# Where a gate, a residual and the conditioning dot products are computed in a macaron layer

## The chip, the cores and the metric

The kernel runs on one core of a Trainium2 chip. The metric is the time of one execution in microseconds (us). Before the change it is 1509.61 us, the median of three runs (1508.7 to 1509.68). The engines have these names in the profile: PE multiplies matrices (PEld is its weight load), DVE is the vector engine, ACT the scalar engine, POOL the GpSimd engine, and SP issues most of the DMA transfers. Each engine carries out its own list of instructions in order; an instruction that waits holds up what stands behind it in its list.

## The reference

512 latent tokens `x` and 256 context tokens `ctx`, 1024 channels each, go through a half-step SwiGLU network (FFN1), then two mixers (neighbourhood attention and a gated delta network), then a second half-step network. Each step is modulated by a conditioning vector:

```python
mod_x = (jax.nn.silu(c) @ w_ada + b_ada).reshape(bsz, N_MOD, 1, d)       # 9 vectors of 1024
mod_c = (jax.nn.silu(c_ctx) @ w_ada + b_ada).reshape(N_MOD, 1, d)

def ffn_sublayer(h, m, i, w_up, w_down):
    shift, scale, gate = sub_mod(m, i)
    y = swiglu(modulate(h, shift, scale), w_up, w_down)
    return post_ln(DEEPNORM_ALPHA * h + 0.5 * gate * y, ln_g[i], ln_b[i])

x = ffn_sublayer(x, mod_x, 0, ffn1_w_in, ffn1_w_out)
ctx = ffn_sublayer(ctx, mod_c, 0, ffn1_w_in, ffn1_w_out)
```

What the change touches is how the modulation vectors (`silu(c) @ w_ada`) get computed beside other work, and where `ALPHA * h + 0.5 * gate * y` is formed for FFN1.

## The kernel before

All weights are fp32 in memory. A weight tile of 128x1024 (512 KB) is loaded into a raw buffer `wr` (or `ra`, `rb`), rounded by ACT to `wh` (line 137, the cast) and its remainder is taken by DVE as `wl` (line 139, the lo half). A product is then three matmuls: `wh` by the high half of the data, `wh` by its low half, `wl` by the high half (lines 192 to 194 for the up products and the projections, 211 for the down products).

The stages, in the order of the trace:

- **FFN1 x**: the first units of the up product, 512 tokens wide, to about 112 us.
- **FFN1 c**: the same units for the context, 256 tokens wide (loop `for f in range(N1)` with `ffn_unit`), 118 to 169 us.
- **down1 x, down1 c**: the first part of the down product for 4 tiles of latent tokens and 2 of context tokens (`down`), to 234.6 us. Its sums leave PSUM in the loop at lines 574 to 590: for each token tile the tokens are loaded, DVE multiplies the two banks with the gate (line 588) and adds ALPHA times the tokens (line 589), and the result is stored to `accd`.
- **Seven**: the remaining 14 units of the up product, x and c together, as 7 block products each (class `Seven`). `prep_a` splits the block `ra` (for products 1 and 2), `prep_s` forms sums of `ra` and `rb` (for 5 and 6, and 3 after `prep_3`), `prep_b` the difference (for 7 and 4). The halves of `prep_a` live in the pool `wx` with one buffer each: the next unit's can be written only when products 1 and 2 of this unit have read them. To about 440 us.
- **down2 x, down2 c**: the rest of the down product; `evac1` adds the sums to `accd` read back as `accx` and `x1c`. To about 563 us. FFN1's layer norms (`finish1`) lie beside down2 c.
- **projections**: first four units of `z`, 512 wide, to 589 us, then units of the mixers to 740 us; then scans, attention and FFN2.

The conditioning vectors are dot products: `ada_gen` loads a 512 KB row block of `w_ada` transposed and DVE multiplies it by a row of silu(c) and sums it (line 280, `dot_cols`), once for `x` and, for the sections 2 to 4, once more for `c`. One `ada_step` is one such load with its one or two dots. The raw buffers of these loads come from the rings of the stage, `raw1` in FFN1 and down1, `raw2` in Seven, a pool `ada1` of four buffers in down2 x. In all there are 48 steps in sections 2 to 7: 10 lie in FFN1 x, FFN1 c and down1 x, 25 in Seven (`ADA2`), the last 13 in down2 x (`ADA3`). When a section is done `rows_out` transposes gates to rows and stores them; the gate of FFN1 (section 2) must be there before down1's sums leave PSUM.

A scheduler lays the program's statements out into each engine's list, so that the order in the lists differs from that of the code; `issue_after` only keeps an instruction behind a named one. The weight stream `Stream` uses the pool `wp` with two raw buffers `wr`, two `wh` and two `wl`; Seven's `rb` is one of the same two raw buffers.

## Time and profile before

| | us |
|---|---|
| median of three runs | 1509.61 |
| the profiled execution's own time | 1512.61 |
| its span from the first to the last instruction | 1510.8 |
| PE busy | 1441.6 |
| DVE busy | 1149.5 |
| ACT busy | 662.8 |

The profiled execution is 3.0 us longer than the median and 1.8 us longer than its own span. In the views, one row is one instruction or a few equal ones beside each other: start, length, engine, line, operation, what it writes and reads, and in brackets how long the engine was idle just before it and what ended that. A matmul's own length includes the time in which it overlaps the next one, so the cadence is read from starts.

### The profile page before, as it was taken

To read this page: it belongs to the slowest core of one execution; us is meant where nothing else is said; L and a number is where in the kernel's file an instruction comes from. 1 tells how busy PE (TensorE), PEld (TensorE's weight loads), DVE (VectorE), ACT (ScalarE), POOL (GpSimd) and SP (SyncE) were. 2 spreads that over 40 slices of the span, in tenths; PEclk is the share of its full clock that TensorE was granted. 3 is DMA by queue.
4 is the path that set the end of the run, shared out by engine and by line. 5 is a ranking of instruction groups with operands and counts; after the bars stand their busy time and mean duration, and the time that the engine had idled before them with its cause. 6 is when DMAs were issued, how large, how long until landed. Compare 5 with 4: busy or idle time off the path is not lost.

```text
span 1510.8 us, 23895 instructions
## 1 busy us (share of the span) xinstructions
PE 1441.6 (95%) x9117; PEld 1262.9 (84%) x9117; DVE 1149.5 (76%) x1975; ACT 662.8 (44%) x1090; POOL 211.2 (14%) x262
## 2 busy tenths in 40 slices
PE   6998999999999989999996998989999999999997
PEld 4778989999997778889875777867778999998886
DVE  8787869999988665778677795567669699886626
ACT  5433524434333386555534334267526454444310
POOL 1000000000000110313201001333221022220001
PEclk9999999999999999999998999999999999999999
DMA  9677664445469444222576514274344143233732
GB/s 375 207 262 232 209 236 171 156 164 167 165 231 397 157 153 134 92 78 91 175 214 183 168 64 124 72 261 146 100 168 144 60 136 107 98 112 121 269 98 83
DMA packets 114948, 248.56 MB, mean 165 GB/s; under 512 B 35145, under 2 KB 50577, under 8 KB 114833
## 3 DMA queue, kind: packets, MB, share of 16 engines
q1 hardware_dynamic: 110192, 229.40, 45.4%
q0 software_dynamic: 3056, 12.33, 2.2%
q10 hardware_dynamic: 1586, 5.32, 0.9%
q8 instruction: 71, 1.16, 0.3%
q14 instruction: 43, 0.35, 0.1%
HBM read 215.50 MB, written 31.50 MB: 163 GB/s over the span
## 4 chain that ended last, share of the span: by engine, by line
PE 69%; DVE 13%; DMA 10%; issue 4%; ACT 3%; POOL 1%; SPq 1%; DVEq 0%; ACTq 0%; POOLq 0%
PE ps L211 15%; PE ps L533 4%; PE ps L535 4%; PE ps L534 4%; PE pm L192 4%; PE pm L193 4%; PE pm L194 4%; PE ps L193 3%; PE ps L192 3%; PE ps L1679 3%; PE ps L194 3%; PE ps L1680 3%; PE ps L1681 3%; PE pc L1049 2%; DVE wl L139 2%
## 5 line engine op out<-in xcount | busy, mean ns | idle before, releaser
L139 DVE TENSOR_TENSOR wl<-wr,wh 128x1024 fp32r<-128x1024 f32 (+1 forms) x184 | 226.8, 1238 | 119.2 <-ACT wh L137 119.0
L137 ACT CAST wh<-wr 128x1024 fp32r<-128x1024 f32 (+1 forms) x184 | 185.9, 1015 | 265.7 <-PE pm L193 60.1
L192 PE MATMUL pm<-uxh,wh 128*128 128x512 f32 x320 | 132.4, 414 | 1.0 <-ACT spill L798 1.0
L194 PE MATMUL pm<-uxh,wl 128*128 128x512 f32 x320 | 127.2, 397 | 0.3 <-DVE wl L139 0.3
L193 PE MATMUL pm<-uxl,wh 128*128 128x512 f32 x320 | 127.1, 397 | 0.0
L211 PE MATMUL ps<-wh,hx 128*128 128x512 f32 x352 | 96.1, 391 | 0.9 <-ACT wh L137 0.9
L211 PEld LDWEIGHTS ps<-wh,hx 128*128 128x128 f32 x352 | 65.9, 188 | 15.3 <-ACT wh L137 1.3
L280 DVE SCALAR_TENSOR_TENSOR adap<-wr,crow 128x1024 f32<-128x1024 f32 x61 | 74.6, 1223 | 2.3 <-DMA wr<-in_w_adaT_dram 1.7
L192 PE MATMUL ps<-uh,wh 128*128 128x256 f32 (+1 forms) x208 | 68.6, 331 | 5.0 <-ACT wh L137 5.0
L194 PEld LDWEIGHTS pm<-uxh,wl 128*128 128x128 f32 x320 | 61.1, 191 | 14.3 <-DVE wl L139 1.3
L192 PEld LDWEIGHTS pm<-uxh,wh 128*128 128x128 f32 x320 | 61.5, 192 | 12.6 <-ACT spill L798 1.4
L193 PEld LDWEIGHTS pm<-uxl,wh 128*128 128x128 f32 x320 | 61.4, 192 | 10.6
L114 POOL TENSOR_TENSOR rs<-ve,mhalf 128x1 f32<-128x1 f32 (+2 forms) x46 | 48.2, 1050 | 140.7 <-DVE ve L110 138.3
L193 PE MATMUL ps<-ul,wh 128*128 128x256 f32 (+1 forms) x208 | 67.5, 326 | 0.0
L194 PE MATMUL ps<-uh,wl 128*128 128x256 f32 (+1 forms) x208 | 66.6, 325 | 0.0
L193 PE MATMUL ps<-uxl,wh 128*128 128x256 f32 (+1 forms) x192 | 61.6, 324 | 2.1 <-DVE uxl L139 2.1
L192 PE MATMUL ps<-uxh,wh 128*128 128x256 f32 (+1 forms) x192 | 60.7, 323 | 1.6 <-ACT uxh L137 1.4
L194 PE MATMUL ps<-uxh,wl 128*128 128x256 f32 (+1 forms) x192 | 61.1, 321 | 0.0
L137 ACT CAST wh<-ra 128x1024 fp32r<-128x1024 f32 x31 | 32.6, 1053 | 58.1 <-PE ps L534 20.2
L533 PE MATMUL ps<-ur,wh 128*128 128x384 f32 x168 | 56.5, 336 | 0.0
L534 PE MATMUL ps<-ur,wh 128*128 128x384 f32 x168 | 56.4, 336 | 0.0
L533 PE MATMUL ps<-uh,wh 128*128 128x384 f32 x168 | 56.4, 336 | 0.0
(498 smaller groups left out, 4264.4 us busy)
## 6 DMA issues: line engine op xcount, KB each, us to landing
wr<-in_w_adaT_dram SPq DMA_DIRECT2D x64, 512.0 KB, 4.8
wr<-in_up_dram SPq DMA_DIRECT2D x56, 512.0 KB, 3.7
wr<-in_win_dram SPq DMA_DIRECT2D x52, 512.0 KB, 3.4
wr<-in_dn_dram SPq DMA_DIRECT2D x51, 512.0 KB, 4.0
ra<-in_up_dram SPq DMA_DIRECT2D x24, 512.0 KB, 4.2
rb<-in_up_dram SPq DMA_DIRECT2D x18, 512.0 KB, 3.3
ra<-in_w_adaT_dram SPq DMA_DIRECT2D x16, 512.0 KB, 5.0
wr<-in_w_o_dram SPq DMA_DIRECT2D x8, 512.0 KB, 4.5
```

The costliest lines, as they stand in the source:

```text
L114: G.tensor_tensor(rs[:], ve[:], mhalf[:, 0:n], ALU.pow)
L137: S.copy(hi, src)
L139: marks["lo"] = V.tensor_tensor(lo, src, hi.bitcast(F32), ALU.subtract).ins
L192: T.matmul(ps, a, uh[:, k, :], start=(k == 0), stop=False)
L193: T.matmul(ps, a, ul[:, k, :], start=False, stop=False)
L194: marks["mm"] = T.matmul(ps, b, uh[:, k, :], start=False, stop=(k == nk - 1)).ins
L211: T.matmul(banks[t][d][:, c0:c1], a[:, sl], b[:, d * 512 + c0:d * 512 + c1], start=first and j == 0, stop=last and j == 2)
L280: V.scalar_tensor_tensor(pr[:], raw[:], 1.0, crow, op0=ALU.mult, op1=ALU.mult, accum_out=col[:, c:c + 1])
L533: T.matmul(ps[:], a, mh, start=k == 0, stop=False)
L534: T.matmul(ps[:], a, ml, start=False, stop=False)
L535: T.matmul(ps[:], b, mh, start=False, stop=k == 3)
L1679: T.matmul(ps[:], a, uh[:, k], start=k == 0, stop=False)
```

## The change

Three things change together.

1. The sums of down1 leave PSUM by two plain ACT copies for a token tile and go to `accd` without gate and residual. The blend (`acc*gate`, then `ALPHA*tokens + that`, two DVE instructions over 1024 columns) is done where they are read back: four token tiles in down2 x, in `h_next`, and two context tiles in down2 c, in `between`, whose tokens are loaded there.
2. The 48 steps are spread otherwise: none in FFN1 x and FFN1 c, two in down1 x, six in down1 c (`t_dots`), 18 in Seven (`ADA2`), 8 in down2 x (`ADA3`), and the last 14 in the projections: two after each `z` unit, then one after every second unit. There the raw buffers are the weight stream's own two (`wp`, `wr`), and the row is a broadcast copy `arow`.
3. The gate's row is stored in the fifth unit of Seven; `ada1` has two buffers in place of four.

```diff
-    ADA2 = (2, 1, 2, 1, 2, 1, 2, 2, 2, 2, 2, 2, 2, 2)
-    ADA3 = (2, 2, 2, 2, 2, 2, 2, 2)
+    ADA2 = (2, 1, 1, 2, 1, 1, 2, 1, 1, 2, 1, 1, 1, 1)
+    ADA3 = (1,) * 8
...
         for k in range(KC * (f - F0), min(KC * (f - F0 + 1), KT)):
             modulate_k(pp, "c", k)
-        ada_step(1 + (f == N1 - 1))
...
         ffn_unit(tp, pp, ws.get(), ws.get(), uch, ucl, NCT, *hc[-1])
-        ada_step(f in (0, 2))
-    rows_out(tp, "fs", 2)
...
-        if j == 0:
-            load_g(0)
+
+    def t_dots(j):
+        if j > 1:
+            ada_step()
...
     for kind, n, hs in (("x", 4, hx), ("c", 2, hc)):
-        if kind == "c":
-            load_g(1)
-        banks, tail = down(pp, ws, hs, n, 2 if kind == "x" else 0, tail if kind == "c" else (), between=t_sums if kind == "x" else None)
+        banks, tail = down(pp, ws, hs, n, 2 if kind == "x" else 0, tail if kind == "c" else (), between=t_sums if kind == "x" else t_dots)
...
-            nc.sync.dma_start(xr, tok_src(kind, t))
-            tmp = tl(tp, [P, D], "adap")
             for d in range(2):
-                sl = slice(d * 512, (d + 1) * 512)
-                V.tensor_tensor(tmp[:, sl], banks[t][d][:], g[d][:], ALU.mult)
-                V.scalar_tensor_tensor(xr[:, sl], xr[:, sl], ALPHA, tmp[:, sl], op0=ALU.mult, op1=ALU.add)
+                S.copy(xr[:, d * 512:(d + 1) * 512], banks[t][d][:])
             nc.gpsimd.dma_start(accd[t + 4 * (kind == "c")], xr)
...
         ada_step(ADA2[f], "h")
+        if f == 4:
+            with tc.issue_after(marks["mm"]):
+                rows_out(sgp, [8, P], "row")
...
-        if j > 3:
+        if 0 < j < 5:
+            xrs.append(tl(ad, [P, D], "xr", 3))
             with tc.issue_after(marks["raw"]):
-                nc.sync.dma_start(accx[j - 4][:], accd[j - 4])
+                nc.sync.dma_start(accx[j - 1][:], accd[j - 1])
+                nc.sync.dma_start(xrs[j - 1][:], tok_src("x", j - 1))
+        if 2 < j < 7:
+            blend(accx[j - 3], xrs[j - 3], gx)
         ada_step(ADA3[j])
 
+    def blend(acc, tok, g):
+        with tc.issue_after(marks["lo"]):
+            V.tensor_tensor(acc[:], acc[:], g[:], ALU.mult)
+            V.scalar_tensor_tensor(acc[:], tok[:], ALPHA, acc[:], op0=ALU.mult, op1=ALU.add)
...
-    ada_tp[0], ada_raw[0] = ad, lambda: tl(ad, [P, D], "wr", 4)
+    ada_tp[0], ada_raw[0] = ad, lambda: tl(ad, [P, D], "wr", 2)
...
-    for _ in ada:
-        pass
...
     def between(j):
+        if j in (4, 7):
+            t = j // 7
+            raw = tl(wp, [P, D], "wr", WB)
+            nc.sync.dma_start(raw[:], tok_src("c", t))
+            blend(x1c[t], raw, gc)
...
+    arow = tl(ga_, [P, D], "arow")
+    nc.gpsimd.dma_start(arow[:], sild.broadcast_to([P, D]))
+    rows_of[0], ada_raw[0] = lambda w: arow[:], lambda: tl(wp, [P, D], "wr", WB)
...
     for m in range(4):
         for _ in fill_spill(ga_, "z", m, zd):
             pass
+        ada_step(2)
...
             if 0 <= j - lag < len(units):
                 next(units[j - lag], None)
+        if j % 2:
+            ada_step()
```

How the lists of the engines change is shown at three places. A row has its place in the engine's list, the line of the kernel it belongs to (lines of the changed kernel are up to ten further on than those of before), the operation, what it writes and reads, and what it waits for besides its place.

**DVE, from the end of down1 c into the first unit of Seven, before.** `ra_2140`, `wr_2141` are the blocks `ra`, `rb` of the first unit, `ra_2144` is `ra` of the second; `s_1649` are the sums; 514, 515, 520 and 525 form them.

```order
257 L514 TENSOR_TENSOR s_1649<-wr_2141 128x512 [waits DMAHW6_49]
258 L139 TENSOR_TENSOR wl_2095<-ra_2092,wh_2094 128x1024 [waits DMAHW0_49,Activation_49]
259 L139 TENSOR_TENSOR wl_2113<-ra_2110,wh_2112 128x1024 [waits DMAHW2_49,Activation_49]
260 L515 TENSOR_TENSOR s_1649<-s_1649,ra_2140 128x512 [waits DMAHW0_49,DVE_49]
...
263 L139 TENSOR_TENSOR wl_2149<-ra_2140,wh_2148 128x1024 [waits Activation_49]
264 L139 TENSOR_TENSOR wl_2155<-s_1649,wh_2154 128x1024 [waits Activation_49]
...
274 L139 TENSOR_TENSOR wl_2225<-ra_2144,wh_2224 128x1024 [waits PE_49,Activation_49]
```

The same place after: `ra_2094`, `wr_2095` belong to the first unit, `ra_2098` to the second; 280 is a dot.

```order
233 L139 TENSOR_TENSOR wl_2103<-ra_2094,wh_2102 128x1024 [waits DMAHW6_49,Activation_49]
234 L280 SCALAR_TENSOR_TENSOR adap_2070,colx_72<-wr_2068,crow_83 128x1024 [waits DMAHW4_49,DVE_49]
235 L280 SCALAR_TENSOR_TENSOR adap_2072,colc_73<-wr_2068,crow_83 128x1024 [waits DVE_49]
...
240 L139 TENSOR_TENSOR wl_2171<-ra_2098,wh_2170 128x1024 [waits DMAHW1_49,PE_49,Activation_49]
241 L515 TENSOR_TENSOR s_1589<-wr_2095 128x512 [waits DMAHW3_49]
242 L516 TENSOR_TENSOR s_1589<-s_1589,ra_2094 128x512 [waits DVE_49]
243 L526 TENSOR_TENSOR wr_2095<-ra_2094,wr_2095 128x512
244 L521 TENSOR_TENSOR s_1589<-ra_2094,s_1589 128x512 [waits DVE_49]
245 L139 TENSOR_TENSOR wl_2109<-s_1589,wh_2108 128x1024 [waits Activation_49]
```

The second unit's `prep_a` (row 240, before row 274) has come ahead of the first unit's sums and of their lo half; row 240 waits, through its cast on ACT, for PE's products 1 and 2 of the first unit.

**PE at the same place after.** Product 2 (`ps_2157`) reads `wh_2102`; the products 5 and 6 (`ps_2174`, `ps_2188`) are the next in the list.

```order
1130 L534 MATMUL ps_2157<-uh_88,wh_2102 128x384
1131 L535 MATMUL ps_2157<-ul_89,wh_2102 128x384
1132 L536 MATMUL ps_2157<-uh_88,wl_2103 128x384
1133 L534 MATMUL ps_2174<-ur_1634,wh_2108 128x384 [waits Activation_49]
1134 L535 MATMUL ps_2174<-ur_1634,wh_2108 128x384
1135 L534 MATMUL ps_2188<-ur_1637,wh_2108 128x384
```

Nothing stands between the last matmul of product 2 and the first that needs the sums.

**SP and DVE in the `z` units, after.** `wr_5248` is the weight of the last `z` unit, `wr_5289` and `wr_5354` those of the next two units; 298 and `in_w_adaT` are loads for dots. The two buffers alternate, so `wr_5242` and `wr_5248` have the same one. First SP:

```order
216 L298 DMA wr_5242<-in_w_adaT_dram 128x1024 [waits DMAHW5_49,DVE_49]
...
226 L806 DMA zd_5141<-spill_5279 128x512 [waits DMAHW1_49,DVE_49]
227 L174 DMA wr_5248<-in_win_dram 128x1024 [waits DMAHW2_49,DVE_49]
228 L298 DMA wr_5283<-in_w_adaT_dram 128x1024 [waits DMAHW3_49,DVE_49]
...
230 L298 DMA wr_5286<-in_w_adaT_dram 128x1024 [waits DMAHW5_49,DMAHW2_49,DVE_49]
231 L174 DMA wr_5289<-in_win_dram 128x1024 [waits DMAHW6_49,DVE_49]
```

Then DVE, where 805 is the end of a `z` unit's sums, 887 a row of the mixers' constants and 280 the dots:

```order
634 L805 SCALAR_TENSOR_TENSOR spill_5279<-spill_5279,ps_5254 128x512 [waits Activation_49]
635 L887 TENSOR_SCALAR aex_5187<-aex_5187 128x8 [waits Activation_49]
636 L280 SCALAR_TENSOR_TENSOR wr_5242,colx_72<-wr_5242,arow_5205 128x1024 [waits DMAHW7_49,DMASW7_49]
637 L280 SCALAR_TENSOR_TENSOR wr_5245,colx_72<-wr_5245,arow_5205 128x1024 [waits DMAHW2_49]
...
639 L805 SCALAR_TENSOR_TENSOR spill_5320<-spill_5320,ps_5295 128x512 [waits DMAHW0_49,Activation_49]
640 L139 TENSOR_TENSOR wl_5251<-wr_5248,wh_5250 128x1024 [waits DMAHW2_49,PE_49,Activation_49]
641 L280 SCALAR_TENSOR_TENSOR wr_5283,colx_72<-wr_5283,arow_5205 128x1024 [waits DMAHW3_49,DVE_49]
```

The last `z` unit's weight is loaded behind the first of the two dots (row 636) that read its buffer, and that dot stands behind rows 634 and 635. Before, these weights followed one another in SP's list with no load for a dot between them.

More of the change, by code (lines that the diff above doesn't have):

```diff
@@ L288, in spread_crow, with ada_gen @@
             S.activation(r[:, w, d * 512:(d + 1) * 512], ps[d][:], AF.Silu)
-    def ada_gen(tps, raw_of, crow):
+    rows_of = [lambda w: crow[:, w]]
+    def ada_gen(tps, raw_of):
         for sec in range(2, 8):
@@ L298, in ada_gen @@
                     for w, col in which:
-                        dot_cols(tps[0], raw, crow[:, w], col, sec * 8 + k, sec > 4)
+                        dot_cols(tps[0], raw, rows_of[0](w), col, sec * 8 + k, sec > 4)
                 if k < KT - 1:
@@ L444, in body, with rows_out @@
     ada_tp, ada_raw, rows_due = [tp], [raw1], []
-    ada = ada_gen(ada_tp, ada_raw, crow)
-    def rows_out(p, tag, bufs):
+    ada = ada_gen(ada_tp, ada_raw)
+    def rows_out(p, shape, *tag):
         while rows_due:
-            to_row(tl(p, [P, 512], tag, bufs)[0:8, 0:P], pp, *rows_due.pop(0))
+            to_row(tl(p, shape, *tag)[0:8, 0:P], pp, *rows_due.pop(0))
     def ada_step(n=1, behind="lo"):
@@ L534, in product @@
                 T.matmul(ps[:], a, ml, start=False, stop=False)
-                T.matmul(ps[:], b, mh, start=False, stop=k == 3)
+                marks["mm"] = T.matmul(ps[:], b, mh, start=False, stop=k == 3).ins
             return ps[:]
@@ L565, in body @@
     sraw = [tl(tp, [P, 3, 512], "s")[:].rearrange("p a n -> p (a n)")]
-    g = []
-    def load_g(w):
-        g[:] = [tl(tp, [P, 512], "fs", 2) for _ in range(2)]
-        row = gates[(w, 2)].rearrange("k p -> (k p)")[None]
-        for d in range(2):
-            nc.sync.dma_start(g[d][:], row[:, d * 512:(d + 1) * 512].broadcast_to([P, 512]))
     for kind, n, hs in (("x", 4, hx), ("c", 2, hc)):
-        if kind == "c":
-            load_g(1)
-        banks, tail = down(pp, ws, hs, n, 2 if kind == "x" else 0, tail if kind == "c" else (), between=t_sums if kind == "x" else None)
+        banks, tail = down(pp, ws, hs, n, 2 if kind == "x" else 0, tail if kind == "c" else (), between=t_sums if kind == "x" else t_dots)
         if kind == "c":
@@ L694, in h_next @@
         h_split_c(2 * j + 2)
-        if j > 3:
+        if 0 < j < 5:
+            xrs.append(tl(ad, [P, D], "xr", 3))
             with tc.issue_after(marks["raw"]):
-                nc.sync.dma_start(accx[j - 4][:], accd[j - 4])
+                nc.sync.dma_start(accx[j - 1][:], accd[j - 1])
+                nc.sync.dma_start(xrs[j - 1][:], tok_src("x", j - 1))
+        if 2 < j < 7:
+            blend(accx[j - 3], xrs[j - 3], gx)
         ada_step(ADA3[j])
+    xrs = []
+    def blend(acc, tok, g):
+        with tc.issue_after(marks["lo"]):
+            V.tensor_tensor(acc[:], acc[:], g[:], ALU.mult)
+            V.scalar_tensor_tensor(acc[:], tok[:], ALPHA, acc[:], op0=ALU.mult, op1=ALU.add)
     ad, close_ad = pool("ada1")
-    ada_tp[0], ada_raw[0] = ad, lambda: tl(ad, [P, D], "wr", 4)
+    ada_tp[0], ada_raw[0] = ad, lambda: tl(ad, [P, D], "wr", 2)
     h_split(4)
@@ L718, in body @@
     nms = [evac1(lp, bx[t], accx[t], accx[t], gx) for t in range(4)]
-    rows_out(lp, "h1", 2)
+    rows_out(lp, [P, 512], "h1", 2)
     gc = tl(lp, [P, D], "g")
@@ L889, in decay @@
         T.transpose(pt[:], gcum[:].rearrange("p d s h -> p (d s h)"), ident)
-        row = tl(ga_, [48, P], "row")
-        S.copy(row[:], pt[:])
-        nc.sync.dma_start(gcd, row[:])
+        row = tl(ga_, [P, 2, P], "vcs")[0:48, 0]
+        S.copy(row, pt[:])
+        nc.sync.dma_start(gcd, row)
         ps = tl(pg, [P, 2, 24], "pg", 5)
```

## The prediction

> **What bounds the kernel now.** First the page's engines' busy times and the chain that ended last.
>
> ```profile
> PE 1441.6 (95%) x9117; PEld 1262.9 (84%) x9117; DVE 1149.5 (76%) x1975; ACT 662.8 (44%) x1090; POOL 211.2 (14%) x262
> PE 69%; DVE 13%; DMA 10%; issue 4%; ACT 3%; POOL 1%; SPq 1%; DVEq 0%; ACTq 0%; POOLq 0%
> ```
>
> PE is busy for 95% of the span. DVE time that is saved where PE does not wait is worth nothing, and the change adds and removes no matmul beyond a few transposes. So the question is only where PE waits now, and where it will wait. Next the busy times by stage (columns: stretch, its length, busy time of PE, PEld, DVE, ACT, POOL with instructions, granted clock, DMA share, GB/s).
>
> ```profile
> 112.00:169.00 57.00, 52.76 (x406) 50.91 (x407) 41.47 (x61) 23.93 (x37) 0.00 (x0) 0.97 0.69 224
> 212.00:234.60 22.60, 22.60 (x102) 18.71 (x101) 14.32 (x17) 7.39 (x7) 1.07 (x2) 1.00 0.61 210
> 234.60:440.00 205.40, 205.40 (x1182) 205.23 (x1181) 195.87 (x309) 81.03 (x107) 8.12 (x15) 1.00 0.49 165
> 440.00:517.00 77.00, 76.14 (x333) 62.03 (x332) 52.53 (x87) 22.77 (x35) 3.49 (x5) 1.00 0.83 307
> 517.00:563.00 46.00, 43.49 (x202) 34.50 (x200) 32.34 (x58) 36.79 (x67) 9.37 (x15) 1.00 0.46 163
> 589.00:740.00 151.00, 150.64 (x943) 134.57 (x942) 112.83 (x176) 88.44 (x151) 43.50 (x45) 1.00 0.30 97
> ```
>
> PE loses 4.2 us in FFN1 c (112 to 169 us), 2.5 in down2 c (517 to 563), under 1 in down2 x (440 to 517) and nothing in down1 c, Seven and nearly nothing in the projections. In Seven (234.6 to 440) DVE is busy for 195.87 of 205.40 us, but PE never waits, so fewer dots there gain nothing.
>
> **A: FFN1 c loses its steps.** PE's waits there, the matmuls behind the longest, and the cast and the SP row that answer to it:
>
> ```profile
> 112.18 0.39 PE L192 MATMUL ps<-uh,wh 128*128 128x256 f32 x1 [0.96 <-ACT wh L137]
> 122.74 0.51 PE L192 MATMUL ps<-uh,wh 128*128 128x256 f32 x1 [2.42 <-ACT wh L137]
> 125.98 0.41 PE L193 MATMUL ps<-ul,wh 128*128 128x256 f32 x1
> 126.20 0.32 PE L194 MATMUL ps<-uh,wl 128*128 128x256 f32 x1
> 126.35 0.28 PE L192 MATMUL ps<-uh,wh 128*128 128x256 f32 x1
> 126.47 0.28 PE L193 MATMUL ps<-ul,wh 128*128 128x256 f32 x1
> 135.27 0.39 PE L192 MATMUL ps<-uh,wh 128*128 128x256 f32 x1 [1.09 <-ACT wh L137]
> ...
> 121.64 1.05 ACT L137 CAST wh<-wr 128x1024 fp32r<-128x1024 f32 x1 [2.43 <-DMA wr<-in_up_dram]
> ...
> 114.28 0.33 SPq L296 DMA_DIRECT2D ra<-in_w_adaT_dram  x1
> 117.40 8.04 SPq L174 DMA_DIRECT2D wr<-in_up_dram  x3
> ```
>
> PE waits for the cast, the cast for a weight whose load was issued at 117.40, behind a dot's load at 114.28: the steps hold the raw buffers. These three idle rows are 0.96 + 2.42 + 1.09 = 4.47 us. Behind 2.42 us of idling a matmul comes every 0.22 us (125.98 to 126.20), and from there every 0.12 (126.35 to 126.47): about half the clock from 122.74 to 126.2, 3.4 us of which 1.5 are lost. Together 6.0 us. Whether they go is read from the dots in the stage (two instructions each in this view: length, DVE busy on line 280, clock, DMA):
>
> ```profile
> 112.00:140.00 28.00, 9.82 (x16) 0.94 0.72 230
> 140.00:169.00 29.00, 2.46 (x4) 1.00 0.66 217
> ```
>
> From 140 to 169, with two dots, no row shows a wait; up to 140 there are eight. So **-6.0 us**; from -7 (some small waits besides) to -4 (the load of the next weight may be late without the dot too).
>
> [...]
>
> **B: from down1 c into Seven.** DVE's new order lets the second unit's lo half (row 240) go ahead of the first unit's sums. Row 240 needs a cast that needs products 1 and 2 of the first unit, and the products after these need the sums. What PE does there now, and the lengths of what it will wait for:
>
> ```profile
> 238.73 0.34 PE L533 MATMUL ps<-ur,wh 128*128 128x384 f32 x1
> ...
> 229.51 0.69 DVE L515 TENSOR_TENSOR s<-s,ra 128x512 f32<-128x512 f32 x1 [0.59 <-DMA ra<-in_up_dram]
> 230.12 0.69 DVE L525 TENSOR_TENSOR wr<-ra,wr 128x512 f32<-128x512 f32 x1
> 233.18 1.23 DVE L139 TENSOR_TENSOR wl<-s,wh 128x1024 fp32r<-128x1024 f32 x1 [0.63 <-ACT wh L137]
> ...
> 238.76 1.05 ACT L137 CAST wh<-ra 128x1024 fp32r<-128x1024 f32 x1 [1.08 <-PE ps L534]
> ```
>
> Product 5 starts at 238.73 with no wait (the row has no bracket), since its lo half was begun at 233.18. After the change the path from the end of product 2 is: cast of the second `ra` 1.05, its lo half 1.22, two sums at the cadence 0.61 (229.51 to 230.12), cast of the sums 1.05, together **4.5 us** of idling, and 3.4 us at half clock behind it, 1.7. Also the `rb` load of the first unit is issued only when a down1 c dot (row 235) has read the same buffer: about 237.8 (the lo half before it, two dots), landing 3.7 later at about 241.5, where the sums could have begun at 241.0:
>
> ```profile
> L280 DVE SCALAR_TENSOR_TENSOR adap<-wr,crow 128x1024 f32<-128x1024 f32 x61 | 74.6, 1223 | 2.3 <-DMA wr<-in_w_adaT_dram 1.7
> wr<-in_w_adaT_dram SPq DMA_DIRECT2D x64, 512.0 KB, 4.8
> wr<-in_up_dram SPq DMA_DIRECT2D x56, 512.0 KB, 3.7
> wr<-in_win_dram SPq DMA_DIRECT2D x52, 512.0 KB, 3.4
> wr<-in_dn_dram SPq DMA_DIRECT2D x51, 512.0 KB, 4.0
> ```
>
> That is 0.5 more: **+6.7**, from 4.5 (clock kept) to 8.5 (the load at the 4.8 of a dot's, and its buffer late). The evacuation itself is no term: DVE loses 24 instructions of 512 columns, about 15 us at 0.6, and gains 12 dots of 1.22; both lie in a stage where PE did not wait. ACT's twelve copies, at a 512-wide 0.6, fit into its 7.39 of 22.6 us.
>
> **C: Seven and down2 x.** Fewer dots in Seven (18 steps for 25), and two 8-row transposes of the gate there, under a PE that does not wait: 0. In down2 x five steps leave, four token loads come, and four blends of about 2.4 us (two 1024-wide instructions, priced as the lo half) against five dots of 1.22: DVE +3.5 us in 77 with 24 free; two buffers serve eight loads of 4.8 in 77 us. The one wait there is 0.86:
>
> ```profile
> 478.12 2.14 PE L211 MATMUL ps<-wh,hx 128*128 128x512 f32 x8 [0.86 <-ACT wh L137]
> ```
>
> It may go or grow: **0**, from -0.9 to +2.
>
> **D: down2 c.** The two context tiles now pass through the weight stream's two raw buffers, each held until its blend has read it. A weight lasts PE 12 matmuls of 0.23 (two of them from 536.74 to 537.20 in the rows below), 2.7 us; a buffer's round is load 4.0, cast 1.05, lo half 1.22, so with two buffers one weight in 3.1 us: a ring already short, that lives from a lead. The lead now, DVE's end against PE's first use:
>
> ```profile
> 531.91 1.22 DVE L139 TENSOR_TENSOR wl<-wr,wh 128x1024 fp32r<-128x1024 f32 x1 [0.36 <-ACT wh L137]
> 537.91 1.23 DVE L139 TENSOR_TENSOR wl<-wr,wh 128x1024 fp32r<-128x1024 f32 x1 [1.37 <-ACT wh L137]
> ...
> 536.74 0.62 PE L211 MATMUL ps<-wl,hc 128*128 128x512 f32 x2
> 537.20 0.62 PE L211 MATMUL ps<-wh,hc 128*128 128x512 f32 x2
> 540.36 0.62 PE L211 MATMUL ps<-wl,hc 128*128 128x512 f32 x2
> ```
>
> The first has 536.74 - 533.13 = 3.6 us to spare, the second 1.2. A context tile ahead of a weight in the same buffer costs that buffer a round of about 6.3 us (load 4.0, two blend instructions of 1.22); the first lo half, 6.3 later, less the 1 that its buffer is idle now, would end near 538.4, about 2 late, and the next ones 0 to 1 late. **+3**, from 0 (the lead covers it) to +5.
>
> **E: the first projections.** The steps' loads alternate with the weights in those two buffers. The last `z` weight waits for a dot's load, its dot, and what stands ahead of that dot. The rows of before:
>
> ```profile
> 577.18 1.28 ACT L878 ACT_TABLE_LOAD   x1
> 578.48 0.21 ACT L878 ACTIVATE aex<-aex 128x8 f32<-128x8 f32 x1
> 579.54 0.58 ACT L798 ACTIVATE spill<-ps 128x512 f32<-128x512 f32 x1
> ...
> 575.92 1.15 ACT L644 ACTIVATE sq<-x1c,nm 128x1024 f32<-128x1024 f32 x1 [2.47 <-DVE nm L655]
> ```
>
> With T as the end of PE's second `z` unit, the new order gives: spill copy to T+0.6; the square and the table load behind it to T+3.1; the constant and DVE's row 635 to T+3.5; the dot to T+4.8; the weight's load, 3.4, to T+8.3; its cast to T+9.4. PE runs dry at T+5.5 (24 matmuls of 0.23). **3.9 us** of idling and 1.7 of half clock, and 0.4 at the next weight, whose buffer waits for two dots: **+6**, from 2 (the ACT part done early, clock kept) to 9 (loads at 4.8). After that one step in two units is 3 raw loads in 11 us or more, and PE's rounds leave room: 0, with DVE at 112.83 of 151 us.
>
> [...]
>
> **Sum.** Against the profiled run's own 1512.61: -6.0 + 6.7 + 0 + 3 + 6 = +9.7, so 1522.3. The median is 3.0 lower than that run: 1509.61 + 9.7 = 1519.3. A wait that comes first gives the loads behind it time, so of the small terms (0.5 in B, 0.4 in E) I leave out 0.8 and take 1518.5.
>
> **Rivals.** (1) The new waits are hidden, A stands: 1509.61 - 6.0 = 1503.6. For it: D and E are races of loads, with prices from busier stages; against it: B is a matter of order, not of speed. Chance 0.17. (2) A and B cancel, D and E hide: 1510.3; or A is worth 4 and one more wait is small. Chance 0.15. (3) The other side, worse than forecast: the ring of two is short in the units of the projections too, which decides once a dot's round (3.4 to 4.8 plus 1.22) is not done within the two 256-wide units of 24 matmuls at 0.12, 2.8 us each; six such steps at 1.5 us make 1518.5 + 9 = 1527.5. Against it: 589 to 740 has a DMA share of 0.30 and DVE is free for 38 us. Chance 0.14. (4) The steps aren't what stalls FFN1 c, and A is 0: 1518.5 + 6.0 = 1524.5. Against it the SP rows above. Chance 0.06. My forecast, 1513 to 1523: 0.48.
>
> **The numbers.** Changes under 0.2%, 3 us, can't be told from none. Faster than 1506.6 is rival 1 and a little more, 0.19; within, rival 2, 0.15; slower the rest, 0.66. The range holds 0.8: from 1504.5, with most of rival 1 in it, to 1525.5, with rival 4 and half of what lies above the forecast.
>
> **What would show it.** A: no idle row over 0.5 us from 112 to 169. B: one idle row of 4 to 5 us on PE's first matmul of product 5, near 232 on the new scale, and half clock behind it. D: waits on casts in down2 c. E: an idle row of about 4 us on the last `z` unit. The forecast falls if B's row is missing, or if the mixers' scans, whose order shifts too, move by more than 3 us.

## The result

The changed kernel takes 1528.98 us (median of 4 runs, 1527.08 to 1530.94) beside 1509.15 for the kernel before (4 runs, 1505.78 to 1509.68): ratio **1.0136, 95% interval 1.0116 to 1.0156**, about 20 us slower. The prediction said 1518.5, in a range to 1525.5.

The profile after, busy times and chain:

```profile
PE 1443.7 (94%) x9117; PEld 1263.0 (83%) x9117; DVE 1146.4 (75%) x1963; ACT 668.0 (44%) x1102; POOL 217.6 (14%) x263
PE 63%; DVE 13%; DMA 12%; issue 6%; ACT 3%; POOL 2%; SPq 1%; DVEq 0%; ACTq 0%; POOLq 0%
```

PE is 2.1 us busier and the span 18.3 us longer: the time came as waits. In the chain PE's share fell from 69 to 63%, and DMA and issue rose by 2 points each. The same view by stage as in the prediction, each stretch here from the first matmul of a stage to that of the next (stretch, length, PE, PEld, DVE, ACT, POOL, granted clock, DMA share, GB/s):

```profile
118.25:163.48 45.23, 45.23 (x385) 45.23 (x384) 26.58 (x33) 21.75 (x32) 0.00 (x0) 1.00 0.54 179
207.03:444.31 237.28, 228.76 (x1275) 224.10 (x1274) 214.65 (x333) 91.46 (x122) 8.62 (x16) 0.98 0.46 163
444.31:527.48 83.17, 79.05 (x339) 64.00 (x338) 56.26 (x89) 26.41 (x40) 4.67 (x8) 0.98 0.73 268
527.48:576.26 48.78, 45.07 (x203) 35.62 (x201) 34.82 (x52) 36.43 (x67) 10.71 (x14) 0.97 0.49 165
576.26:624.16 47.90, 40.87 (x186) 32.70 (x184) 30.51 (x51) 24.66 (x43) 4.62 (x17) 0.96 0.55 182
```

FFN1 c has no wait left; the four other stages of this view each have. Both kernels were profiled a second time. Lengths of the stages in us, read in the same way in each trace. FFN1 c begins at the first 256-wide matmul behind the last 512-wide one of FFN1 x; the row ahead of it takes in everything up to its end. The scans' second part begins at the first product that reads `r` and ends at the first transpose of `oacc`:

| stage | before | before, again | after | after, again | prediction's term |
|---|---|---|---|---|---|
| start to the end of FFN1 c | 169.19 | 166.44 | 163.48 | 164.49 | A |
| FFN1 c | 51.41 | 48.99 | 45.23 | 45.23 | A -6.0 |
| down1 x | 43.62 | 43.65 | 43.55 | 43.54 | 0 |
| down1 c with Seven | 226.17 | 226.16 | 237.28 | 236.62 | B +6.7 |
| down2 x | 78.06 | 78.13 | 83.17 | 83.45 | C 0 |
| down2 c | 46.82 | 46.90 | 48.78 | 49.27 | D +3 |
| z to the first conv transpose | 41.65 | 41.50 | 47.90 | 48.49 | E +6 |
| from there to the scans | 207.03 | 209.35 | 211.02 | 214.41 | 0 |
| scans, first part | 51.45 | 50.16 | 52.48 | 53.14 | 0 |
| scans, second part | 107.51 | 106.36 | 102.51 | 101.49 | 0 |

In the first pair the differences of the rows (without FFN1 c, which is part of the row above it) add up to +18.7 us; the span grew by 18.3.

PE's idle rows of the changed kernel in the five stages of the view, the ones over 0.8 us:

```profile
241.91 0.69 PE L534 MATMUL ps<-ur,wh 128*128 128x384 f32 x1 [8.52 <-ACT wh L137]
473.30 2.11 PE L211 MATMUL ps<-wh,hx 128*128 128x512 f32 x8 [1.58 <-ACT wh L137]
477.94 1.18 PE L211 MATMUL ps<-wl,hx 128*128 128x512 f32 x2 [2.54 <-DVE wl L139]
548.87 1.42 PE L211 MATMUL ps<-wh,hc 128*128 128x512 f32 x4 [2.78 <-ACT wh L137]
561.86 1.20 PE L211 MATMUL ps<-wh,hc 128*128 128x512 f32 x4 [0.87 <-ACT wh L137]
597.45 0.79 PE L192 MATMUL ps<-uxh,wh 128*128 128x512 f32 x1 [4.70 <-ACT wh L137]
614.16 0.50 PE L192 MATMUL pm<-uxh,wh 128*128 128x512 f32 x1 [0.96 <-ACT wh L137]
```

The row of B is where it was expected, at the first matmul of product 5, but of 8.52 us in place of 4.5. The two rows of down2 x were not expected. Who ended them is read one step further back. At the border of down1 c and Seven, the loads and stores around 231 and what DVE did (SP, POOL, then DVE rows):

```profile
229.96 0.33 SPq L298 DMA_DIRECT2D wr<-in_w_adaT_dram  x1
231.82 2.86 SPq L502 DMA_DIRECT2D wr<-in_up_dram  x2
...
230.19 0.53 POOL L577 DMA_DIRECT2D accd<-hx  x1 [21.29 <-ACT hx L576]
231.17 0.53 POOL L577 DMA_DIRECT2D accd<-hx  x1 [0.45 <-ACT hx L576]
...
234.47 1.22 DVE L139 TENSOR_TENSOR wl<-ra,wh 128x1024 fp32r<-128x1024 f32 x1
239.36 0.69 DVE L515 TENSOR_TENSOR s<-wr 128x512 f32<-128x512 f32 x1 [3.67 <-DMA wr<-in_up_dram]
```

The second unit's lo half, which the prediction made the cause, is done at 235.69. Then DVE waits 3.67 us for the `rb` load, issued at 231.82 and landed 7.5 us later: a dot's load, the context's two stores and the second `rb` load (issued at 234.35) are in flight with it, each for a part of that time. The busy times of two microseconds in that wait show no engine computing, the granted clock at 0.50 and a share of the 16 DMA engines of 1.02:

```profile
236.00:238.00 2.00, 0.00 (x0) 0.00 (x0) 0.00 (x0) 0.00 (x0) 0.00 (x0) 0.50 1.02 410
```

In down2 x, the cast and DVE's list at that time:

```profile
472.20 1.04 ACT L137 CAST wh<-wr 128x1024 fp32r<-128x1024 f32 x1 [0.88 <-DMA wr<-in_dn_dram]
...
471.44 1.22 DVE L698 TENSOR_TENSOR ax<-ax,g 128x1024 f32<-128x1024 f32 x1
472.58 1.22 DVE L280 SCALAR_TENSOR_TENSOR wr<-wr,crow 128x1024 f32<-128x1024 f32 x1
473.72 1.23 DVE L699 SCALAR_TENSOR_TENSOR ax<-xr,ax 128x1024 f32<-128x1024 f32 x1
474.86 0.76 DVE L139 TENSOR_TENSOR hc<-hc 128x256 fp32r<-128x256 f32 x2
475.53 1.22 DVE L699 SCALAR_TENSOR_TENSOR ax<-xr,ax 128x1024 f32<-128x1024 f32 x1
476.67 1.22 DVE L139 TENSOR_TENSOR wl<-wr,wh 128x1024 fp32r<-128x1024 f32 x1
```

The cast is done at 473.24; its lo half begins at 476.67, behind the rest of a dot, the second instructions of two blends and two short lo halves of `hc` (0.7 us) that stand ahead of it in DVE's list. That is the 2.54 us row.

### The profile page after: what moved, and what is told of

Same layout as the page of the kernel before. It is cut to its first block, busy times and chain, and to the rows that moved or that the text cites. A ratio compares the mean times of both kernels' runs of the same rounds, so it can differ in the third digit from the quotient of the medians.

```text
span 1529.1 us, 23857 instructions
## 1 busy us (share of the span) xinstructions
PE 1443.7 (94%) x9117; PEld 1263.0 (83%) x9117; DVE 1146.4 (75%) x1963; ACT 668.0 (44%) x1102; POOL 217.6 (14%) x263
## 4 chain that ended last, share of the span: by engine, by line
PE 63%; DVE 13%; DMA 12%; issue 6%; ACT 3%; POOL 2%; SPq 1%; DVEq 0%; ACTq 0%; POOLq 0%
PE ps L211 10%; PE ps L534 4%; PE ps L536 4%; PE ps L535 4%; PE pm L192 4%; PE pm L194 4%; PE pm L193 4%; PE ps L1691 3%; PE ps L1690 3%; PE ps L1692 3%; PE ps L194 3%; PE ps L192 3%; PE ps L193 3%; DVE wl L139 3%; PE pc L1060 2%
## 5 line engine op out<-in xcount | busy, mean ns | idle before, releaser
L114 POOL TENSOR_TENSOR rs<-ve,mhalf 128x1 f32<-128x1 f32 (+2 forms) x46 | 46.5, 1011 | 138.8 <-DVE ve L110 136.4
L211 PE MATMUL ps<-wl,hx 128*128 128x512 f32 x176 | 55.9, 396 | 2.5 <-DVE wl L139 2.5
L536 PE MATMUL ps<-ur,wl 128*128 128x384 f32 x168 | 56.7, 339 | 0.0
```

The costliest lines, as they stand in the source:

```text
L114: G.tensor_tensor(rs[:], ve[:], mhalf[:, 0:n], ALU.pow)
L211: T.matmul(banks[t][d][:, c0:c1], a[:, sl], b[:, d * 512 + c0:d * 512 + c1], start=first and j == 0, stop=last and j == 2)
L536: marks["mm"] = T.matmul(ps[:], b, mh, start=False, stop=k == 3).ins
```

## The experiments

The chip's level differed between the sets of runs (the median of before lay between 1509 and 1518 us), so ratios to the runs of before on the same chip are compared; the changed kernel's is 1.0136 (1.0116 to 1.0156). Where the interval of a run overlaps this one, the total shows no difference, and only the stages of its profile speak. A trace is of one execution.

**1. No steps in down1 c.**

```diff
-        banks, tail = down(..., between=t_sums if kind == "x" else t_dots)
+        banks, tail = down(..., between=t_sums if kind == "x" else None)
-    ADA2 = (2, 1, 1, 2, 1, 1, 2, 1, 1, 2, 1, 1, 1, 1)
+    ADA2 = (2, 1, 2, 1, 2, 1, 2, 2, 2, 2, 2, 2, 2, 1)
```

> The changed kernel without the six dot steps in down1 c; they go to Seven, which then has 24 steps. Theory (the steps of down1 c hold the raw buffer and the DMA engines ahead of the first unit's rb load): the 8.5 us idle row at product 5 and the half clock behind it go, Seven with one step less than before the change costs nothing; 1529.0 - 10 = 1519 us (1517 to 1521). Rival (the order of the lists or the context's two stores alone make it): an idle row of 4 us or more stays, 1524 us or more.

Ratio 1.0122 (1.0107 to 1.0138). Down1 c with Seven took 226.62 us, without the idle row: B is gone, whole. But down2 c grew to 52.89 us (waits of 1.67 and 2.82 at casts), and of the 10.7 us the total shows nothing: the interval overlaps that of the changed kernel. That the total would fall by 10 was wrong.

**2. The context's stores later, by a scheduling order.**

```diff
+            with tc.issue_after(marks["lo"]) if kind == "c" else nullcontext():
-            nc.gpsimd.dma_start(accd[t + 4 * (kind == "c")], xr)
+                nc.gpsimd.dma_start(accd[t + 4 * (kind == "c")], xr)
```

> The changed kernel with the context's two stores of partial sums issued only behind the lo half of the first unit's sums. Theory (two stores of 512 KB and a dot's load in flight double the rb load's 3.7 us): rb lands 3.5 to 5 us after its issue in place of 7.5, the idle row at product 5 falls from 8.5 to 5 to 6 us, what the order of the lists alone gives; about 1526 us. Rival (buffer held by the dots, stores harmless): idle row 8 to 9 us, 1529 us.

1.0147 (1.0131 to 1.0164); idle row 8.47 us. It tells nothing: the order names an instruction of DVE, the stores are in POOL's list, where nothing else stands near them, and they still went out at 231.22 and 232.20, right behind the copies, ahead of the `rb` load at 232.51. So `issue_after` made no wait here. Run 3 does what this one meant to.

**3. The same stores on SP's list, behind the second unit's `rb` load.**

```diff
-            nc.sync.dma_start(self.rb[:], I["up1"][2 * f + 1])
+            marks["rb"] = nc.sync.dma_start(self.rb[:], I["up1"][2 * f + 1]).ins
...
+                with tc.issue_after(marks["rb"]):
+                    nc.sync.dma_start(accd[4 + t], xr)
```

> The changed kernel with the context's two stores of partial sums on SP's list, behind the second unit's rb load. Theory (the stores slow the rb load): the first unit's rb load lands 4 to 5.5 us after its issue in place of 7.5, the idle row at product 5 falls from 8.5 to 5.5 to 6.5 us; down1 c with Seven 234 to 235.5 us in place of 237.3. Rival (it is the load for the dots and the buffer's late release alone): row of 8 us or more, 237 us.

1.0129 (1.0108 to 1.0149), not to be told from the changed kernel. The stage took 234.66 us, 2.6 less. The rows:

```profile
230.84 2.86 SPq L502 DMA_DIRECT2D wr<-in_up_dram  x2
...
238.71 0.69 PE L534 MATMUL ps<-ur,wh 128*128 128x384 f32 x1 [6.09 <-ACT wh L137]
...
235.15 0.69 DVE L515 TENSOR_TENSOR s<-wr 128x512 f32<-128x512 f32 x1 [1.61 <-DMA wr<-in_up_dram]
235.76 1.22 DVE L139 TENSOR_TENSOR wl<-ra,wh 128x1024 fp32r<-128x1024 f32 x1
236.90 0.68 DVE L516 TENSOR_TENSOR s<-s,ra 128x512 f32<-128x512 f32 x1
```

With the stores issued 2.9 us behind it (at 233.75 and 234.27), and itself issued 1.0 us sooner, the load lands 4.3 us after its issue. In this list the second unit's lo half stands between the two sums and costs 1.1 us (235.76 to 236.90).

**4. The six steps two weights earlier.**

```diff
     def t_dots(j):
-        if j > 1:
+        if j < 6:
             ada_step()
```

> The changed kernel with the six steps of down1 c at its weights 0 to 5 in place of 2 to 7; in DVE's list the first unit's sums then stand ahead of the second unit's lo half, and its rb load ahead of less. Theory (not the number of steps there but the last two, which hold the raw buffer and go ahead of the rb load, make the idle row): product 5 with an idle row of 0 to 2 us in place of 8.5, down1 c with Seven 226 to 229 us in place of 237.3. Rival (six steps in that stage are too many for DVE and the buffers wherever they stand): idle rows of 5 us or more in sum from down1 c to product 5, 232 us or more.

1.0083 (1.0054 to 1.0111); 228.22 us, with these two rows of PE in place of the 8.52:

```profile
232.65 0.45 PE L534 MATMUL ps<-ur,wh 128*128 128x384 f32 x1 [0.97 <-ACT wh L137]
233.91 0.44 PE L536 MATMUL ps<-ur,wl 128*128 128x384 f32 x1 [0.29 <-DVE wl L139]
```

Not the number of steps but the place of the last two made B: they hold the raw buffers of the weight stream until the stage is nearly over, and the `rb` load is issued only then. Here it went out at 225.06, ahead of the context's stores (228.47 and 229.45); how much of the gain is the buffer and how much the distance from the stores, only run 3's 2.6 us for the stores tells.

**5. No steps at the z units.**

```diff
-    ADA2 = (2, 1, 1, 2, 1, 1, 2, 1, 1, 2, 1, 1, 1, 1)
+    ADA2 = (2, 1, 2, 2, 2, 2, 2, 2, 2, 2, 2, 2, 2, 1)
...
-        ada_step(2)
```

> The changed kernel without the eight dot steps at the z units; they go to Seven, which then has 26 steps. Theory (in the first projections the weight stream's two raw buffers are shared with the dots): the 4.7 us idle row at the last z unit and the half clock go, 1529.0 - 6 = 1523 us (1521 to 1525). Rival (Seven's DVE, 95% busy, is pushed over its limit by eight more steps): Seven grows by 3 to 8 us and eats the gain, 1526 to 1531 us.

1.0070 (1.0052 to 1.0089), some 10 us better than the changed kernel by the ratios. From z to the first conv transpose 43.86 us in place of 47.90, from there to the scans 208.32 in place of 211.02. The 4.70 us row is gone, but a wait of another kind has come, for ACT's `u` at the unit behind the last `z` unit:

```profile
608.96 0.79 PE L192 MATMUL pm<-uxh,wh 128*128 128x512 f32 x1 [3.25 <-ACT u L151]
```

Since the border of the two stages moves with the order of the list, their sum is the safer measure. It is 258.0 to 262.9 us in the nine profiles with the `z` steps, 248.7 to 252.4 in the six without any step in the projections, and 252.2 in this run, which still has six steps in the later units: the `z` steps cost some 6 to 11 us, and of the six others no cost is seen. Seven, with 26 steps, did not grow (236.09 with B's row still in it).

**6. No steps in either place, one behind each unit.**

```diff
-        ada_step(2)
...
-        if j % 2:
-            ada_step()
+        ada_step()
```

(with experiment 1's edit)

> The changed kernel with no steps in down1 c and at the z units: Seven has 24, and the units behind z one each until the 14 left are done. Theory (B and E come from the steps at those two places, each time from the buffers shared with the weights): down1 c with Seven 226 to 227 us, from z to the first conv transpose 43 to 44.5 us (47.9 in the changed kernel), the later projections no longer than there (211 us); ratio 1.002 to 1.005 of before, C and D remaining. Rival (the shared ring costs in the later units too): those grow by 5 us or more, ratio 1.007 or more.

1.0095 (1.0080 to 1.0111). Down1 c with Seven took 226.61 us. From z to the scans it is 257.1 us, beside 252.2 in experiment 5 with six steps in the units, and 258.9 and 262.9 in the changed kernel's two profiles. The ratio is the rival's, not the theory's 1.002 to 1.005: fourteen steps in the units cost some 5 us more than six. That is little above the scatter of this sum (4.0 us between the two profiles of the changed kernel), and the two ratios' intervals overlap, so the size is not sure.

**7 and 8. The blends of the latent tiles left out; then their token loads too.** Gate and residual of FFN1 for x are not applied in these two.

```diff
-        if 2 < j < 7:
-            blend(accx[j - 3], xrs[j - 3], gx)
...
-                nc.sync.dma_start(xrs[j - 1][:], tok_src("x", j - 1))
```

> The changed kernel with the blends of the four latent token tiles left out (gate and residual of FFN1 for x are not applied); their loads stay. Theory (DVE works off the blends ahead of the weight's lo half): the 2.5 us idle row of down2 x at a lo half goes, the 1.6 us one at a cast stays or shrinks, and down2 x falls from 83.2 to 79 to 80.5 us; 1525 to 1526 us. Rival (the token loads and the stores read back, not the blends): both idle rows stay, down2 x at 82.5 to 83.5 us, 1529 us.

> The changed kernel with the blends of the four latent token tiles and the loads of their tokens left out (gate and residual of FFN1 for x are not applied). Theory (in down2 x the blends hold the lo half on DVE, 2.2 us, and the token loads hold the weights, the rest): down2 x 77.5 to 79 us (78.1 before, 83.2 in the changed kernel, 81.0 with the loads alone). Rival (the earlier and bunched read-back of the partial sums holds the weights, not the tokens): 80.5 us or more.

Down2 x took 80.99 and 77.53 us, in place of 83.17 (ratios 1.0114, 1.0099 to 1.0130, and 1.0082, 1.0061 to 1.0103). Without the blends the wait at the lo half is gone and that at the cast stays, longer than the 1.58 it was:

```profile
474.94 3.43 PE L211 MATMUL ps<-wh,hx 128*128 128x512 f32 x8 [2.23 <-ACT wh L137]
```

Without the token loads no idle row of 0.5 us or more is left in the stage. So C is 2.2 us of the blends in DVE's list and 3.5 us of loads. Which wait shows them depends on the order: in runs 1, 5 and 6 the stage has one wait of 2.9 to 4.2 us, at a cast, and none at a lo half, with nearly the same length (81.7 to 83.5 us). In the first part of the stage the DMA share is 1.02 and 1.03 (last but one column), in the changed kernel:

```profile
450.00:456.00 6.00, 6.00 (x28) 4.96 (x27) 2.60 (x6) 0.81 (x2) 0.00 (x0) 1.00 1.02 414
456.00:462.00 6.00, 6.00 (x28) 4.98 (x27) 2.57 (x5) 2.50 (x4) 0.00 (x0) 1.00 1.03 415
```

and 0.99 and 1.00 in the kernel before:

```profile
450.00:456.00 6.00, 6.00 (x28) 4.97 (x27) 3.37 (x6) 4.16 (x9) 0.00 (x0) 1.00 0.99 363
456.00:462.00 6.00, 6.00 (x28) 4.96 (x27) 5.36 (x12) 0.13 (x1) 0.00 (x0) 1.00 1.00 381
```

The kernel before shows there, from 450 to 480 us, what a load of 512 KB takes under such a share, here the weights and the partial sums read back (median from issue to landing):

```profile
wr<-in_dn_dram SPq DMA_DIRECT2D x5, 512.0 KB, 6.9
ax<-accd SPq DMA_DIRECT2D x4, 512.0 KB, 8.7
```

**9. The blends and tokens of the context left out.** Gate and residual of FFN1 for ctx are not applied.

```diff
-        if j in (4, 7):
-            t = j // 7
-            raw = tl(wp, [P, D], "wr", WB)
-            nc.sync.dma_start(raw[:], tok_src("c", t))
-            blend(x1c[t], raw, gc)
```

> The changed kernel with the blends of the two context tiles and the loads of their tokens left out (gate and residual of FFN1 for ctx are not applied). Theory (the two tiles take rounds of the weight stream's two raw buffers): down2 c 46.5 to 47.5 us in place of 48.8 to 52.9, no idle row over 1.5 us at a cast. Rival (down2 c suffers from what down2 x leaves late): 48.5 us or more.

Down2 c took 47.17 us; the largest wait at a cast was 0.60 us. D is the two tiles; loads in the weights' raw buffers and blends were left out together, so their shares were not told apart. The ratio, 1.0119 (1.0088 to 1.0149, 2 runs), shows no gain; in this profile z to the first conv transpose took 53.69 us.

**10. The evacuation alone.** The kernel before with the deferred gate and residual; every dot step where it was.

> The kernel before with only the evacuation changed (plain ACT copies in down1, blends in down2 x and down2 c, tokens of the context through the weight stream's raw buffers); the dot steps stay where they were. Theory (the deferred blends cost in down2 x and down2 c, and free nothing that PE waits for in down1): FFN1 c stays at 51.4 us, down1 c with Seven at 226 us, down2 x 80 to 83 us (78.1 before), down2 c 48.5 to 53 us (46.8 before); 1.003 to 1.007 of before. Rival (the blends in down2 only cost beside fewer steps and two buffers; alone the change is neutral or a gain since DVE is freed in down1): 0.998 to 1.001.

1.0118 (1.0098 to 1.0137): by itself it costs nearly what the whole change costs, and more than theory and rival had. FFN1 c and down1 c with Seven are as before (226.19 us). Down2 x took 89.02 us, 11 more than before and 6 more than the theory's most, with 13 steps, four token loads and four blends in it; down2 c 49.58. Its waits are those of C, larger:

```profile
472.18 3.78 PE L211 MATMUL ps<-wh,hx 128*128 128x512 f32 x8 [4.45 <-ACT wh L137]
490.66 1.21 PE L211 MATMUL ps<-wl,hx 128*128 128x512 f32 x2 [2.84 <-DVE wl L139]
```

The changed kernel has five steps fewer in this stage, and its C is 5 us. That these five make the difference was not tested by itself.

**11. The two steps of FFN1 c moved into FFN1 x**, evacuation as before.

```diff
-        ada_step(1 + (f == N1 - 1))
+        ada_step(2 if f < F0 + 3 else 1)
...
-        ada_step(f in (0, 2))
```

> The kernel before with the two dot steps of FFN1 c moved into FFN1 x (two steps in each of its first three units, one in the last two; evacuation as before). Theory (the steps' loads in FFN1 c hold the weights' raw buffers): FFN1 c falls from 51.4 to 45.2 to 46.5 us, nothing else moves, 0.9965 of before (about -5 us). Rival (the steps at the end of FFN1 x, not those in c, hold the first context weights): FFN1 c stays at 50 us or more, or FFN1 x grows by as much; 0.999 to 1.001.

1.0018 (1.0003 to 1.0033). The theory's fall came, and the rival's growth too. With the border of the table FFN1 c took 45.0 us (129.22 to 174.22) and has no wait, as the theory said. But FFN1 x ended at 129.22 in place of 117.78, 11.4 us later, with these rows; the matmul of the first takes 0.79 us, as long as the one at 597.45 us in the changed kernel, where the clock was 0.51:

```profile
105.71 0.79 PE L192 MATMUL ps<-uh,wh 128*128 128x512 f32 x1 [4.80 <-ACT wh L137]
120.77 0.50 PE L192 MATMUL ps<-uh,wh 128*128 128x512 f32 x1 [1.76 <-ACT wh L137]
```

So the two steps of FFN1 c make its waits, and put into FFN1 x they cost more there: FFN1 c ends 5.0 us later than in the first profile of before.

**12 and 13. The eight steps kept away from the border of x and c**, evacuation as before. In 12, `ada_step(f < N1 - 1)` in x and `ada_step(f in (3, 4, 5, 6))` in c; in 13, `f < N1 - 2` and `f in (2, 3, 4, 5, 6)`.

> The kernel before, evacuation as before, with the eight steps of the first gate placed otherwise: one in each unit of FFN1 x but the last, one in each of the units 4 to 7 of FFN1 c. Theory (the three steps about the border of x and c hold the raw buffers for the first context weights; a step later in c is harmless, since two dots there met no wait): FFN1 c 45.2 to 46.5 us in place of 51.4, 0.996 to 0.9975 of before. Rival (any step in c costs): 49 us or more, 0.999 to 1.001.

> As the run before, with none in the last two units of FFN1 x and one in each of the units 3 to 7 of FFN1 c. Theory: as there, 45.2 to 46.5 us, 0.996 to 0.9975; it is better by what the fourth unit's step cost at the border. Rival (any step in c costs): 50 us or more.

**0.9960 (0.9946 to 0.9975) and 0.9962 (0.9947 to 0.9977)**: both faster than the kernel before by some 6 us, the best ones of the study, and in the range that the theory gave. FFN1 c took 47.73 and 48.69 us, more than its 45.2 to 46.5; in 12 these rows are the waits over 0.5 us at its border and in it:

```profile
112.45 0.39 PE L192 MATMUL ps<-uh,wh 128*128 128x256 f32 x1 [0.73 <-ACT wh L137]
165.65 0.27 PE L242 MATMUL ps<-ident,colc 128*8 128x128 f32 x1 [2.17 <-DVE colc L303]
```

The waits behind the border are gone; the gate's transpose now waits for the last dot, 2.17 us (1.98 in 13). FFN1 c ends at 165.68 and 164.94 us, beside 169.19 and 166.44 in the two profiles of before, so 0.8 to 4.3 us of the 6 are there. Both parts of the scans together took 157.2 and 152.9 us (159.0 and 156.5 in before). Where the rest lies can't be told from one profile each.

**14 and 15. Both kernels profiled again.**

> The kernel before, profiled once more. Theory (the 4 us by which the projections are longer and the 4 us by which what follows is shorter in the changed kernel are the scatter of one execution): the stage from the first conv transpose to the scans' first product lies between 206 and 213 us and the scans' second part between 100 and 108 us, at least one of them over 2 us from its first profile (207.0 and 107.5). Rival (they are the change's doing, by the order of the lists): both within 1 us of the first profile.

> The changed kernel, profiled once more. The stages that the prediction priced come again within 0.7 us: FFN1 c 45.2, down1 c with Seven 237.3, down2 x 83.2, down2 c 48.8, from z to the first conv transpose 47.9; what scatters more (down2 c is the candidate, it lay between 47.2 and 52.9 in the runs) can't be priced from one profile.

The table at the head has the lengths. The stages priced in the prediction came again within 0.7 us, but for FFN1 c of the kernel before, 2.4 us shorter the second time. The stretch to the scans scatters by 2.3 and 3.4 us, as the theory of run 14 had it, and is longer in the changed kernel both times. The scans' second part does not scatter so: 106 to 107.5 in before (and 107.42 in run 10, whose lists are nearest to it), 100 to 104 in every other kernel. In run 11, which differs from before in FFN1 alone, much of DVE's list far behind it stands in another order, and this part took 102.55 us. So the 5 us gained there probably come with the order of the lists; which order it is was not looked for. Part of it is lost again in the scans' first part, which is 50 to 51.5 us in before and in run 10 and 52 to 55.5 in the others; both parts together are 4.0 and 1.9 us shorter in the changed kernel.

## Why the prediction was wrong

**The sign held, and so did the mechanisms of A, B, D and E. But B's load was priced at half of what it took, C and the later projections were put at nothing and cost 5 us and 4 to 5 us, and the total lay 3.5 us above the range.**

**A, -6.0:** in FFN1 c -6.2 against the first profile, -3.8 against the second. The 0.96 us row lies ahead of this stage's border, in FFN1 x, where the changed kernel has waits of its own (0.64 and 0.59 at lo halves). Up to the end of FFN1 c the pairs differ by -5.7 and -2.0: 166.4 to 170.5 us in the three profiles with the FFN1 of before, 162.0 to 164.9 in the eleven with the changed one. Right in mechanism (steps' loads hold the raw buffers, run 11). That late steps in c cost little was not seen; runs 12 and 13 show it.

**B, +6.7:** measured +11.1 and +10.5. One term of the sum was mis-sized. The prediction charged 4.5 us for the order of the lists, 0.5 for the `rb` load that comes behind it, and 1.7 for the clock. Measured are 4.85 us (8.52 less DVE's wait for the load), 3.67, and a clock of 0.50 for 4.0 us behind the row (241.91 to 245.92). The load was issued when the prediction had it: 237.8 us, less the 6.0 of A, is 231.8, and it went out at 231.82. But its landing was priced with the median of its kind, 3.7 us, while up to four other transfers of 512 KB were in flight; it took 7.5, and 4.3 where the context's stores came later (run 3). The stores, which come at once when ACT makes its four copies in 2.06 us (230.19 and 231.17; 237.70 for the first of them before), were no term at all. With the load as late as this the order costs nothing more, since the sums would have waited for it anyway. Moving the steps two weights earlier removes nearly all of B (run 4).

**C, 0:** measured +5.1 and +5.3, and this is the step that failed most. "DVE +3.5 us in 77 with 24 free" is an average over the stage: seven of the eight blend instructions came between 465.8 and 479.0 us, in part ahead of the lo half that PE needed. And five loads gone against four come was an account of bytes over the whole stage; the tokens and the sums are read back in its first 30 us, where the DMA share is about 1.0 before the change too (1.01 from 440 to 470 us). The price of 4.8 us for a load was the median of the whole run; in this part of the stage the trace of before has medians of 6.9 to 8.7. Runs 7 and 8 divide C, 2.2 and 3.5 us.

**D, +3:** measured +2.0 and +2.4; run 9 shows that the two tiles are the cause. In the eleven profiles with these blends the stage took 48.8 to 52.9 us, +2 to +6, so the bound of +5 was too narrow.

**E, +6:** measured +6.3 and +7.0, but the agreement is in part luck. The idle row is 4.70 for 3.9, since the dot also waited for the broadcast row:

```profile
591.80 1.23 DVE L280 SCALAR_TENSOR_TENSOR wr<-wr,arow 128x1024 f32<-128x1024 f32 x1 [0.99 <-DMA arow<-sild]
...
593.06 0.33 SPq L174 DMA_DIRECT2D wr<-in_win_dram  x1
...
597.43 1.23 DVE L139 TENSOR_TENSOR wl<-wr,wh 128x1024 fp32r<-128x1024 f32 x1 [0.70 <-ACT wh L137]
```

Load, cast and lo half follow the dot as the prediction had them. What it left out is that the first `z` unit already lost time before the change, between two stretches of its view by stage (563 to 589 us): this wait, and 3.4 us at a clock of 0.50 around it (566.57 to 569.99), some 3 us that are gone in the changed kernel.

```profile
566.62 0.79 PE L193 MATMUL ps<-uxl,wh 128*128 128x512 f32 x1 [1.31 <-DVE uxl L139]
```

Against it stand three smaller waits behind the 4.70 us row that were no term (0.53, 0.96 and 0.53).

**The later projections, 0:** "PE's rounds leave room" was said of the six steps behind `z`, and of these no cost is seen (run 5). But the stretch from the first conv transpose to the scans grew by 4.0 and 5.1 us. With the `z` steps away, this stretch and the first projections together are back in the range of the kernels that have no step there (run 5). So by these profiles the `z` steps cost more than E's stage shows, and the prediction let their cost end there. By which waits it goes on was not looked for.

**The rivals.** Rival 3, the ring short in the later units, was given 0.14. Its time came nearly true (1527.5 for 1529.0), its mechanism did not at its six steps; at fourteen steps run 6 bears it out with some 5 us. Rivals 1 and 2 fell with the idle rows of B, D and E; rival 4 fell with A. A move of the scans by more than 3 us, which the prediction named as a sign against itself, came too: their two parts are 4.0 us shorter in the first pair and 1.9 in the second, and no term had it.

**The clock and the table load.** Charging half a clock to B and E was right: in the changed kernel the granted clock was 0.50 for 4.0 us behind the wait of 8.52 us and for 3.41 behind that of 4.70. The lower ends of both ranges had the clock kept; no run shows that behind the rows of B and E, and the changed kernel shows 0.50 there. The clock was 0.50 for 3.41 us also behind the waits of 2.54 and 2.78 us. It was 1.00 behind 1.58, behind 2.17 in run 12 and behind 2.72 at 640.30 us; the last section has rows of two of these. The table load on E's path took the 1.28 us that it took before: in the changed kernel it begins at 589.11, 0.02 us behind the end of the instruction before it, and the next one starts 1.29 us behind its start.

## What to carry to other kernels

Price a load by what is in flight beside it at that moment, stores included, and not by the median of its kind over the run; the trace before the change can have loads under the same share of the DMA engines (here the down weights, 6.9 us at a share of 1.01 from 450 to 480 us, with 4.0 over the run). Stores that slow arithmetic had spaced out came in a burst when the arithmetic was gone: the context's two were issued 5.9 us apart before (237.70 and 243.58) and 1.0 apart after (230.19 and 231.17). An engine's free share over a stage says nothing of an instruction that lands ahead of a needed one in its list (in down2 x DVE was busy for 56.26 of 83.17 us, and PE waited 2.54 us for a lo half): look for the burst, and for the one item that PE waits for next. What extra loads in a two-buffer weight ring cost depended on their place here: with six of them down1 c and Seven took 11 us more when they reached to the end of down1 c, and 2 us more two weights earlier.

## What the runs showed of the hardware

A 512 KB load took 7.5 us from issue to landing with up to four other transfers of that size in flight (DMA share 1.02, 410 GB/s over two microseconds of it), and 4.3 with the two stores issued 2.9 us behind it. Behind a wait of 1.58 us eight matmuls of 512 columns took 2.11 us, at a granted clock of 1.00, and behind 4.45 us they took 3.78 at 0.50. An order that put stores of POOL's list behind a DVE instruction did not delay them (run 2: 231.22 and 232.20 us, ahead of the `rb` load at 232.51).

In the changed kernel's first profile the granted clock was 0.50 for 3.41 us from 478.02, 549.70 and 597.49 us on, behind the waits of 2.54, 2.78 and 4.70 us, and for 10.24 us from 235.68 on, in the wait of 8.52 and behind it. The first three of these starts lie 71.68 and 47.79 us apart, 21 and 14 times 3.41. In the 3.41 us ahead of each of the four PE was idle for 2.54, 2.58, 3.37 and 2.28 us, by its busy time. The wait of 2.54 us lies whole within the 3.41 us ahead of 478.02. The one of 2.72 us does not lie so: 638.45 us, which is 12 times 3.41 behind 597.49, cuts it into 0.87 and 1.85, and the clock behind it was 1.00. That the idle time within one such length counts, and not the length of the wait, is an estimate from these rows (busy time of PE is the first number behind the comma, the clock the third from the end):

```profile
474.61:478.02 3.41, 0.87 (x5) 0.40 (x3) 3.41 (x6) 1.88 (x3) 0.00 (x0) 1.00 1.04 414
478.02:481.43 3.41, 3.41 (x8) 2.70 (x9) 3.41 (x5) 0.62 (x1) 0.00 (x0) 0.50 0.86 304
638.45:641.86 3.41, 1.56 (x14) 1.56 (x15) 3.41 (x5) 2.46 (x5) 3.35 (x1) 1.00 0.11 19
641.86:645.28 3.42, 3.42 (x19) 2.90 (x18) 3.38 (x4) 1.27 (x3) 1.12 (x2) 1.00 0.91 320
```
